# Feed-forward chunks of 12, 12, 10 and 10 blocks, and a pair of fp32 matmuls behind each feed-forward's first norm

## The chip, the core and the metric

The kernel runs on one core of a Trainium2 chip. The metric is the device time of one launch in microseconds. PE is the matrix engine (TensorE; PEld is its weight load), DVE, ACT and POOL are the vector, scalar and GpSimd engines, SP is the engine from whose queue most transfers start.

## The reference

One step of a small hybrid decoder: a prompt of 256 positions and 8 samples of 4 positions, 288 token columns in all, width 2048, all in fp32.

```
x = x + 1/2 * SwiGLU_1(rmsnorm(x))            # FFN1, d_ff = 5632
z = rmsnorm(x) @ w_in                         # mixer: state-space group and attention group
x = x + w_out @ concat(rmsnorm(y_ssm), rmsnorm(y_attn))
x = x + 1/2 * SwiGLU_2(rmsnorm(x))            # FFN2
swiglu(x) = (silu(x @ w_gate) * (x @ w_up)) @ w_down
```

The two feed-forwards, FFN1 and FFN2, are three quarters of the work. Their 5632 hidden columns are 44 blocks of 128.

## The kernel before, in words

Tokens are columns. `x[0..15]` are 16 tiles of 128 x 288, resident. A product of fp32 precision is made of three fast matmuls (fp32r): every weight piece `raw` is split into a high part `wh` (ACT, line 88) and a low part `wl` (DVE, line 89), every activation likewise (`xh`, `xl` of the normed input; `hh`, `hl` of the hidden blocks), and `mm3` issues wh by the high tile (L272), wh by the low tile (L273), wl by the high tile (L274) for each block of 128 rows. So the moving operand goes high, low, high, then on to the next block.

SBUF places are set by the pools. A tile of 288 floats is 1152 bytes per partition. `xh0` to `xh15` lie one behind the other, then the 128-byte tile `gap_x`, then `xl0` to `xl15`. The hidden blocks live in a ring of 14 `hh` tiles and a ring of 14 `hl` tiles, with the 128-byte tile `gap_r` between the two rings.

Order is written by hand. `Weights` streams a list of pieces: 512 KB pieces of gate and up weights (8 blocks, 24 matmuls), and pieces of the down weights. `next()` hands out one piece, a slot: it splits two pieces ahead, issues loads up to five ahead on SP's queue (5 `raw` buffers, 3 each of `wh` and `wl`), and runs whatever other work `at` or `spread` put at that slot, ahead of the slot's matmuls. A feed-forward goes in four chunks: `gu` of 11 blocks (4 pieces each: gate and up, two halves), the first `gu` of the next chunk, then `down` of the chunk: for each of the 16 output tiles d a PSUM tile gets 6 blocks from one piece and 5 from the next, and DVE adds it to x (L327).

The norm is applied late: `Hold` runs it some slots into the feed-forward (`first` is 10 in FFN1, 2 in FFN2): one fp32 matmul of `ones` by the sum of squares `acc` (L206), then DVE computes the row factor `R` (L200), and the evictions held up till then follow one a slot. The PSUM tiles, all named `main`, go round eight banks.

Into FFN1, from slot 24 on, the tables of the state-space part are spread (`precompute`), eight times `tile_tables`: two groups of four transposes (L556), and one or two slots later a pair of fp32 matmuls of 256 columns (L562):

```
for i, xx in ((0, xr), (1, xi)):
    pe.matmul(ps[:, :256], rep[i].rearrange("p q g c -> p (q g c)"), xx[:, :, 1:5, :],
              start=i == 0, stop=i == 1)
```

FFN2 has no such other work. In each feed-forward the slots count 304 pieces.

Of the kernel before, what the change touches and what calls it, by code (L numbers as in the profile page):

```python
# [10 lines left out]
F32 = mybir.dt.float32  # L11
# [6 lines left out]
P = 128  # L18
D = 2048
KT = D // P  # L20
# [5 lines left out]
N = T * W1  # L26
DFF = 5632
NF = DFF // P
CH = 11
NCK = NF // CH  # L30
HALF = 8 * P
EPS = 1e-6
NH = 16
# [8 lines left out]
def heads_of(i):  # L42
    kvp, g = divmod(i, 4)
    return (2 * kvp) * 4 + g, (2 * kvp + 1) * 4 + g
# [72 lines left out]
def tile_hymba_step(ctx, tc, io):  # L117
    nc = tc.nc
    act, dve, pool_e, pe, sp = nc.scalar, nc.vector, nc.gpsimd, nc.tensor, nc.sync
# [5 lines left out]
    pm = ctx.enter_context(tc.tile_pool(name="pm", bufs=8, space=PSUM))  # L125
# [4 lines left out]
    pieces = []  # L130

    def ffn_units(l):
        seq = []
        for c in range(NCK):
            for f in range(CH):
                if not (c > 0 and f == 0):
                    seq.append(("gu", c * CH + f))
            if c + 1 < NCK:
                seq.append(("gu", (c + 1) * CH))
            seq.append(("down", c))  # L140
        return seq

    def ffn_pieces(l):
        gu, dn = io["w_gu%d" % l], io["w_dn%d" % l]
        for kind, j in ffn_units(l):
            if kind == "gu":
                for s in range(2):
                    for hf in range(2):
                        pieces.append(gu[j, s, hf])
            else:  # L150
                for d in range(KT):
                    pieces.append(dn[j, d, :, :6 * P])
                    pieces.append(dn[j, d, :, 6 * P:])

    ffn_pieces(0)
    pieces[:6] = [pieces[i] for i in (0, 2, 4, 1, 3, 5)]
    MIX0 = len(pieces)
# [7 lines left out]
    W = Weights(nc, wp, pieces)  # L165
# [8 lines left out]
    ones = cp.tile([P, P], F32, name="ones")  # L174
    acc = cp.tile([P, N], F32, name="acc")
    R = cp.tile([P, N], F32, name="R")
# [91 lines left out]
    def mm3(ps, wh, wl, kts, rh, rl, first, last):  # L268
        n = len(kts)
        for a, k in enumerate(kts):  # L270
            s = slice(a * P, (a + 1) * P)
            pe.matmul(ps, wh[:, s], rh[k], start=first and a == 0, stop=False)  # L272
            pe.matmul(ps, wh[:, s], rl[k], start=False, stop=False)  # L273
            pe.matmul(ps, wl[:, s], rh[k], start=False, stop=last and a == n - 1)  # L274

    def projs(n):

        ps = [pm.tile([P, 512], F32, name="main") for _ in range(n)]
        for hf in range(2):
            for p_ in ps:  # L280
                wh, wl = W.next()
                mm3(p_[:, :N], wh, wl, range(8 * hf, 8 * hf + 8), xh, xl, hf == 0, hf == 1)
        return ps

    def proj():
        return projs(1)[0]

    def ffn(l, post, hp, first):
        HH, HL = {}, {}
        hold = Hold(W.i + first)  # L290
        early = [] if l else projs(3)

        def gate(f, pg, s2):
            t1 = tp.tile([P, N], F32, name="t1")
            s1 = tp.tile([P, N], F32, name="s1")
            dve.tensor_tensor(t1, pg[:, :N], R, op=ALU.mult)  # L296
            act.activation(s1, t1, AF.Silu)  # L297
            pool_e.tensor_tensor(s2, s1, R, op=ALU.mult)  # L298

        def up(f, pu, s2):  # L300
            h = tp.tile([P, N], F32, name="h")
            hh = hp.tile([P, N], F32R, name="hh")
            if f == 0:
                hp.tile([P, 32], F32, name="gap_r", bufs=1)
            hl = hp.tile([P, N], F32R, name="hl")
            dve.tensor_tensor(h, pu[:, :N], s2, op=ALU.mult)  # L306
            act.copy(hh, h)  # L307
            dve.tensor_tensor(hl, h, hh.bitcast(F32), op=ALU.subtract)  # L308
            HH[f % CH, f // CH], HL[f % CH, f // CH] = hh, hl

        def gu(f):
            s2 = tp.tile([P, N], F32, name="s2")
            pg = early.pop(0) if early else proj()
            hold(lambda: gate(f, pg, s2))
            pu = early.pop(0) if early else proj()
            hold(lambda: up(f, pu, s2))

        def down(c):
            rh = {k: HH.pop((k, c)) for k in range(CH)}
            rl = {k: HL.pop((k, c)) for k in range(CH)}  # L320
            for d in range(KT):
                ps = pm.tile([P, 512], F32, name="main")
                wh, wl = W.next()
                mm3(ps[:, :N], wh, wl, range(6), rh, rl, True, False)
                wh, wl = W.next()
                mm3(ps[:, :N], wh, wl, range(6, CH), rh, rl, False, True)
                dve.scalar_tensor_tensor(x[d], ps[:, :N], 0.5, x[d], op0=ALU.mult, op1=ALU.add)  # L327
                if c == NCK - 1:
                    post(d)

        for kind, j in ffn_units(l):
            (gu if kind == "gu" else down)(j)

# [779 lines left out]
def token_columns(xp, xs):  # L1113

    s = xs[:, ::-1].transpose(1, 0, 2)
    p = xp.reshape(NCH, T, -1)[:, ::-1].transpose(1, 0, 2)
    return np.concatenate([s, p], axis=1).reshape(N, -1)
# [38 lines left out]
def layout(a):  # L1156
    A = {k: np.asarray(v) for k, v in a.items()}
    c = np.ascontiguousarray
    o = {}
    xt = token_columns(A["x_prompt"][0], A["x_sample"])  # L1160
    o["x"] = c(xt.T.reshape(KT, P, N))

    def kblocks(w):

        n = w.shape[1] // P
        return w.reshape(2, 8, P, n, P).transpose(3, 0, 2, 1, 4).reshape(n, 2, P, 8 * P)

    for l, nm in enumerate(("ffn1", "ffn2")):
        g, u = kblocks(A[nm + "_w_gate"][0]), kblocks(A[nm + "_w_up"][0])
        o["w_gu%d" % l] = np.stack([g, u], 1)  # L1170
        w = A[nm + "_w_down"][0].reshape(NCK, CH, P, KT, P)
        o["w_dn%d" % l] = c(w.transpose(0, 3, 2, 1, 4).reshape(NCK, KT, P, CH * P))
    w = A["w_in"][0]
    qcols = np.concatenate([np.r_[64 * h:64 * h + 64] for i in range(8) for h in heads_of(i)])
    cols = np.concatenate([np.arange(2048, 2176), np.arange(1024), np.arange(2176, 2560), 1024 + qcols])
    o["w_in"] = c(kblocks(w[:, cols]))
    w = A["w_out"][0][np.concatenate([np.arange(1024), 1024 + qcols])]
    o["w_out"] = c(w.reshape(2, 8, P, KT, P).transpose(0, 3, 2, 1, 4).reshape(2, KT, P, 8 * P))

    def gcol(v):  # L1180
        return v.reshape(-1, P).T

    o["gains"] = c(np.concatenate(
        [gcol(A["ffn1_norm"][0]), gcol(A["mix_norm"][0]), gcol(A["ffn2_norm"][0]),
         gcol(A["ssm_out_norm"][0]), gcol(A["attn_out_norm"][0][qcols]),
         np.tile(A["q_norm"][0], 2)[:, None], np.tile(A["k_norm"][0], 2)[:, None]], 1))

    def pairs(v):

        return v.reshape((32, 2, 64) + v.shape[2:]).swapaxes(0, 1).swapaxes(1, 2).reshape(  # L1190
            (P, 32) + v.shape[2:])

    dt = np.repeat(A["ssm_log_dt"][0][:, None], 64, 1)
    dco = A["ssm_D"][0].reshape(8, P).T
    o["ssm_prm"] = c(np.concatenate([pairs(A["ssm_A_re"][0]), pairs(A["ssm_A_im"][0]), pairs(dt),
                                     dco], 1))
    o["ssm_bc"] = c(np.stack([pairs(A["ssm_B_re"][0]), pairs(A["ssm_B_im"][0]),
                              pairs(A["ssm_C_re"][0].swapaxes(1, 2)),
                              pairs(A["ssm_C_im"][0].swapaxes(1, 2))], 1))
    o["h0"] = c(np.stack([pairs(A["state_ssm_%s" % r][0].transpose(1, 2, 0)) for r in ("re", "im")], 1))  # L1200
    glu = np.zeros((8, 8, 16, 8, 16), np.float32)
    for g in range(8):
        glu[:, g, :, g, :] = A["ssm_w_glu"][0].reshape(8, 8, 16, 16)[:, g]
    o["w_glu"] = glu.reshape(8, P, P)
    o["ssm_cst"], o["mix_cst"], o["ident"] = constants()
    sk = A["sinks"][0]
    sp_ = np.concatenate([np.r_[sk[list(heads_of(i))], sk[list(heads_of(i))]] for i in range(8)])
    g = (np.arange(P) // 4) % 4
    ss = np.stack([sk[kv * 4 + g] for kv in range(4)], 1)
    o["sinks"] = c(np.concatenate([np.tile(sp_[None], (P, 1)), ss], 1))  # L1210
    o["cache_k"], o["cache_v"] = A["cache_k"], A["cache_v"]
    o["cache_kT"] = c(A["cache_k"][0].reshape(NB, WIN, 2, P).transpose(2, 3, 0, 1))
    o["cache_vr"] = c(A["cache_v"][0].reshape(NB, WIN, 2, P).transpose(2, 1, 0, 3))
    return o
# [44 lines left out]
```

## Time and profile before

| | |
|---|---|
| median of 3 runs | 2023.21 us (2022.99 to 2023.37) |
| the profiled execution: time, span | 2021.75 us, 2020.0 us |
| granted PE clock | 1.00 throughout |
| PE, DVE, ACT, POOL busy | 99%, 60%, 42%, 15% of the span |
| HBM traffic | 178 GB/s over the span |
| FFN1; mixer; FFN2 (PE's first matmul of each) | 6.3; 862.5; 1172.4 us |

The profiled execution's time is 1.75 us more than its span. Everything below is read against that one execution and then carried over to the median, which is 1.5 us higher. A matmul here is shown with a duration of some 0.29 us while the next starts some 0.13 us behind it, so they overlap: what counts is the distance of their starts, which a number of matmuls in a window of known length gives.

### The profile page before, as it was taken

Reading aid. Unit: us, or ns where it says so; the run is one execution under the profiler, and the core shown is the slowest. Engines: PE = TensorE matmul, PEld = TensorE weight load, DVE = VectorE, ACT = ScalarE, POOL = GpSimd, SP = SyncE. Lnnn points to the kernel's source line nnn. Section 1 sums busy time; section 2 is a strip of 40 time slices with the busy share of each in tenths; the row PEclk is TensorE's granted clock in tenths of the full one; section 3 lists DMA queues with packets and bytes.
Section 4 is the critical chain, followed back from the end, with each engine's and each line's share of the span. In section 5 each row is a group of like instructions: output and inputs, shape, how many; then the busy total and the mean of one; then the engine's idle time right before and its main releaser. Section 6 shows DMA issues by size and latency. Waiting matters only on the chain.

```text
span 2020.0 us, 37616 instructions
## 1 busy us (share of the span) xinstructions
PE 2004.1 (99%) x15248; PEld 1992.0 (99%) x15248; DVE 1218.3 (60%) x1874; ACT 852.3 (42%) x1334; POOL 298.8 (15%) x450
## 2 busy tenths in 40 slices
PE   8999999999999999999999999999999999999999
PEld 8999999999999999999989999999999999999999
DVE  5677666666656655677787974455445444454454
ACT  5433443444444433533476543333333333333332
POOL 3100011001110000212477720000000000000000
PEclk9999999999999999999999999999999999999999
DMA  7555656565656564678733555555555655465554
GB/s 237 189 161 151 215 158 200 175 207 163 201 173 197 180 199 147 215 238 273 238 126 127 165 161 165 161 151 182 166 168 146 188 164 162 146 180 170 164 158 149
DMA packets 122622, 359.04 MB, mean 178 GB/s; under 512 B 22448, under 2 KB 30256, under 8 KB 121264
## 3 DMA queue, kind: packets, MB, share of 16 engines
q1 hardware_dynamic: 114672, 340.81, 53.7%
q10 hardware_dynamic: 7776, 15.83, 2.3%
q8 instruction: 119, 1.95, 0.4%
q14 instruction: 55, 0.45, 0.1%
HBM read 338.40 MB, written 20.22 MB: 178 GB/s over the span
## 4 chain that ended last, share of the span: by engine, by line
PE 94%; POOL 2%; DVE 2%; DMA 1%; issue 0%; ACT 0%; SPq 0%; POOLq 0%; ACTq 0%; DVEq 0%
PE main L272 30%; PE main L274 30%; PE main L273 30%; POOL acc L190 1%; PE main L723 1%; DVE wl L89 1%; DMA yd<-yg 0%; PE main L556 0%; PE main L562 0%; DMA x<-in_x 0%; PE main L765 0%; PE main L764 0%; PE main L763 0%; DMA raw<-in_w_gu 0%; POOL rq_t L891 0%
## 5 line engine op out<-in xcount | busy, mean ns | idle before, releaser
L89 DVE TENSOR_TENSOR wl<-raw,wh 128x1024 fp32r<-128x1024 f32 (+2 forms) x680 | 757.8, 1115 | 539.8 <-ACT wh L88 535.6
L272 PE MATMUL main<-xh,wh 128*128 128x288 f32 x3136 | 931.0, 297 | 6.9 <-ACT xh L180 6.3
L274 PE MATMUL main<-xh,wl 128*128 128x288 f32 x3136 | 925.8, 295 | 1.3 <-DVE wl L89 1.3
L273 PE MATMUL main<-xl,wh 128*128 128x288 f32 x3136 | 925.4, 295 | 0.6 <-DVE xl L181 0.6
L88 ACT CAST wh<-raw 128x1024 fp32r<-128x1024 f32 (+2 forms) x680 | 643.0, 946 | 614.1 <-PE main L273 406.9
L272 PEld LDWEIGHTS main<-xh,wh 128*128 128x128 f32 x3136 | 591.9, 189 | 8.1 <-ACT xh L180 6.3
L274 PEld LDWEIGHTS main<-xh,wl 128*128 128x128 f32 x3136 | 591.7, 189 | 2.0 <-DVE wl L89 2.0
L273 PEld LDWEIGHTS main<-xl,wh 128*128 128x128 f32 x3136 | 591.9, 189 | 1.4 <-DVE xl L181 1.0
L272 PE MATMUL main<-hh,wh 128*128 128x288 f32 x1664 | 494.1, 297 | 0.0
L273 PE MATMUL main<-hl,wh 128*128 128x288 f32 x1664 | 490.9, 295 | 0.3 <-DVE hl L674 0.3
L274 PE MATMUL main<-hh,wl 128*128 128x288 f32 x1664 | 491.0, 295 | 0.0
L273 PEld LDWEIGHTS main<-hl,wh 128*128 128x128 f32 x1664 | 313.9, 189 | 0.7 <-DVE hl L674 0.6
L272 PEld LDWEIGHTS main<-hh,wh 128*128 128x128 f32 x1664 | 313.3, 188 | 0.4
L274 PEld LDWEIGHTS main<-hh,wl 128*128 128x128 f32 x1664 | 313.6, 188 | 0.0
L298 POOL TENSOR_TENSOR s<-s,R 128x288 f32<-128x288 f32 x88 | 71.5, 813 | 1253.7 <-ACT s L297 1253.7
L297 ACT ACTIVATE s<-t 128x288 f32<-128x288 f32 x88 | 39.2, 445 | 237.5 <-DVE t L296 237.5
L307 ACT CAST hh<-h 128x288 fp32r<-128x288 f32 x88 | 38.1, 433 | 239.6 <-DVE h L306 239.6
L327 DVE SCALAR_TENSOR_TENSOR x<-main,x 128x288 f32<-128x288 f32 x128 | 58.4, 456 | 51.0 <-PE main L274 49.1
L306 DVE TENSOR_TENSOR h<-main,s 128x288 f32<-128x288 f32 x88 | 40.2, 457 | 77.0 <-PE main L274 76.8
L296 DVE TENSOR_TENSOR t<-main,R 128x288 f32<-128x288 f32 x88 | 40.2, 457 | 63.6 <-PE main L274 63.1
L308 DVE TENSOR_TENSOR hl<-h,hh 128x288 fp32r<-128x288 f32 x88 | 40.4, 459 | 44.0 <-ACT hh L307 44.0
L190 POOL TENSOR_TENSOR acc<-acc,sq 128x288 f32<-128x288 f32 x45 | 48.5, 1079 | 52.5 <-ACT sq L186 51.1
(264 smaller groups left out, 890.1 us busy)
## 6 DMA issues: line engine op xcount, KB each, us to landing
raw<-in_w_gu SPq DMA_DIRECT2D x352, 512.0 KB, 3.5
raw<-in_w_dn SPq DMA_DIRECT2D x128, 384.0 KB, 3.1
raw<-in_w_dn SPq DMA_DIRECT2D x128, 320.0 KB, 2.9
raw<-in_w_in SPq DMA_DIRECT2D x40, 512.0 KB, 4.5
raw<-in_w_out SPq DMA_DIRECT2D x32, 512.0 KB, 3.4
mats<-stage ACTq DMA_DIRECT2D x8, 1536.0 KB, 7.0
mb<-mats SPq DMA_DIRECT2D x8, 768.0 KB, 5.7
ma<-mats SPq DMA_DIRECT2D x8, 512.0 KB, 4.3
```

The lines of the kernel that those rows point to most:

```text
L88: self.nc.scalar.copy(wh[:, :n], t[:, :n])
L89: self.nc.vector.tensor_tensor(wl[:, :n], t[:, :n], wh[:, :n].bitcast(F32), op=ALU.subtract)
L190: eng.tensor_tensor(acc, acc, sq, op=ALU.add)
L272: pe.matmul(ps, wh[:, s], rh[k], start=first and a == 0, stop=False)
L273: pe.matmul(ps, wh[:, s], rl[k], start=False, stop=False)
L274: pe.matmul(ps, wl[:, s], rh[k], start=False, stop=last and a == n - 1)
L296: dve.tensor_tensor(t1, pg[:, :N], R, op=ALU.mult)
L297: act.activation(s1, t1, AF.Silu)
L298: pool_e.tensor_tensor(s2, s1, R, op=ALU.mult)
L306: dve.tensor_tensor(h, pu[:, :N], s2, op=ALU.mult)
L308: dve.tensor_tensor(hl, h, hh.bitcast(F32), op=ALU.subtract)
L327: dve.scalar_tensor_tensor(x[d], ps[:, :N], 0.5, x[d], op0=ALU.mult, op1=ALU.add)
```

## The change

The four chunks have 12, 12, 10 and 10 blocks. A down piece carries half a chunk, 6 or 5 blocks, and lies contiguous in its own array in HBM; before, the pieces were the first 768 and the last 640 columns of rows of 1408. And a function `gap` runs eight slots behind the first norm of each feed-forward: two fp32 matmuls of `ones` by 256 columns of `R` into a PSUM tile that nothing reads.

```diff
-CH = 11
-NCK = NF // CH
+CHS = (12, 12, 10, 10)
+NCK = len(CHS)
+C0 = [sum(CHS[:c]) for c in range(NCK)]
...
             else:
                 for d in range(KT):
-                    pieces.append(dn[j, d, :, :6 * P])
-                    pieces.append(dn[j, d, :, 6 * P:])
+                    pieces.append(dn[j][d, 0])
+                    pieces.append(dn[j][d, 1])
...
     def ffn(l, post, hp, first):
         HH, HL = {}, {}
+        w0 = W.i
         hold = Hold(W.i + first)
...
         def down(c):
-            rh = {k: HH.pop((k, c)) for k in range(CH)}
-            rl = {k: HL.pop((k, c)) for k in range(CH)}
+            n = CHS[c]
+            rh = {k: HH.pop(C0[c] + k) for k in range(n)}
+            rl = {k: HL.pop(C0[c] + k) for k in range(n)}
             for d in range(KT):
                 ps = pm.tile([P, 512], F32, name="main")
                 wh, wl = W.next()
-                mm3(ps[:, :N], wh, wl, range(6), rh, rl, True, False)
+                mm3(ps[:, :N], wh, wl, range(n // 2), rh, rl, True, False)
                 wh, wl = W.next()
-                mm3(ps[:, :N], wh, wl, range(6, CH), rh, rl, False, True)
+                mm3(ps[:, :N], wh, wl, range(n // 2, n), rh, rl, False, True)
...
+        def gap():
+
+            ps = pm.tile([P, 512], F32, name="main")
+            for i in range(2):
+                pe.matmul(ps[:, :256], ones, R[:, 8:264], start=i == 0, stop=i == 1)
+
+        W.at(w0 + first + 8, gap)
```

Lines move by one to ten: `mm3`'s L272 to L274 are L273 to L275 now, the table's L556 and L562 are L566 and L572, the new pair is L338.

Where it stands on PE in FFN2, first the pair. Before, at slot 10 of FFN2 (`xh15` ends a block's second gate piece, `xh0` begins its first up piece; the numbers tell tiles of one name apart):

```order
L272 MATMUL main_14501<-xh15_102,wh_14464 128x288
L273 MATMUL main_14501<-xl15_119,wh_14464 128x288
L274 MATMUL main_14501<-xh15_102,wl_14465 128x288
L272 MATMUL main_14567<-xh0_87,wh_14502 128x288
L273 MATMUL main_14567<-xl0_104,wh_14502 128x288
L274 MATMUL main_14567<-xh0_87,wl_14503 128x288
```

The same place on PE now, with the pair as one row of two:

```order
L273 MATMUL main_14504<-xh15_102,wh_14467 128x288
L274 MATMUL main_14504<-xl15_119,wh_14467 128x288
L275 MATMUL main_14504<-xh15_102,wl_14468 128x288
L338 MATMUL main_14577<-R_124,ones_122 128x256 x2
L273 MATMUL main_14570<-xh0_87,wh_14505 128x288
L274 MATMUL main_14570<-xl0_104,wh_14505 128x288
```

Nothing else moved there: the pair stands between two pieces, ahead of `xh0`.

Second, on PE the seam between output tiles 0 and 1 in the first down of FFN2. Before, `hh_15701` is the chunk's block 10 and `hh_14368` its block 0:

```order
L272 MATMUL main_15840<-hh_15701,wh_15804 128x288
L273 MATMUL main_15840<-hl_15702,wh_15804 128x288
L274 MATMUL main_15840<-hh_15701,wl_15805 128x288
L272 MATMUL main_15887<-hh_14368,wh_15841 128x288
L273 MATMUL main_15887<-hl_14370,wh_15841 128x288
```

Now, on PE at the same seam, `hh_15841` is block 11 and `hh_14371` block 0:

```order
L273 MATMUL main_15980<-hh_15841,wh_15944 128x288
L274 MATMUL main_15980<-hl_15842,wh_15944 128x288
L275 MATMUL main_15980<-hh_15841,wl_15945 128x288
L273 MATMUL main_16030<-hh_14371,wh_15981 128x288
L274 MATMUL main_16030<-hl_14373,wh_15981 128x288
```

An output tile ends on a block with an odd number in its chunk now (11 or 9), where it ended on an even one (10).

Third, on PE in FFN1's last down, behind the pair of the seventh table, whose slot is the same in both. Before, a second half of 5 blocks follows it, from the chunk's block 6 (`hh_6229`) on:

```order
L562 MATMUL main_7386<-xr_6943,rep0_245 128x256
L562 MATMUL main_7386<-xi_6944,rep1_246 128x256
L272 MATMUL main_7349<-hh_6229,wh_7321 128x288
L273 MATMUL main_7349<-hl_6230,wh_7321 128x288
L274 MATMUL main_7349<-hh_6229,wl_7322 128x288
```

Now, on PE, a second half of 5 blocks follows too, but from the chunk's block 5 (`hh_6478`) on:

```order
L572 MATMUL main_7507<-xr_7042,rep0_245 128x256
L572 MATMUL main_7507<-xi_7043,rep1_246 128x256
L273 MATMUL main_7473<-hh_6478,wh_7445 128x288
L274 MATMUL main_7473<-hl_6479,wh_7445 128x288
L275 MATMUL main_7473<-hh_6478,wl_7446 128x288
```

The tables' work keeps its slots; the pieces at these slots are other ones.

More of the change, by code (lines that the diff above doesn't have):

```diff
@@ L134, in ffn_units @@
         for c in range(NCK):
-            for f in range(CH):
+            for f in range(CHS[c]):
                 if not (c > 0 and f == 0):
-                    seq.append(("gu", c * CH + f))
+                    seq.append(("gu", C0[c] + f))
             if c + 1 < NCK:
-                seq.append(("gu", (c + 1) * CH))
+                seq.append(("gu", C0[c + 1]))
             seq.append(("down", c))
@@ L143, in ffn_pieces @@
     def ffn_pieces(l):
-        gu, dn = io["w_gu%d" % l], io["w_dn%d" % l]
+        gu, dn = io["w_gu%d" % l], [io["w_dn%d_%d" % (l, c)] for c in range(NCK)]
         for kind, j in ffn_units(l):
@@ L308, in up @@
             dve.tensor_tensor(hl, h, hh.bitcast(F32), op=ALU.subtract)
-            HH[f % CH, f // CH], HL[f % CH, f // CH] = hh, hl
+            HH[f], HL[f] = hh, hl
         def gu(f):
@@ L1170, in layout @@
         o["w_gu%d" % l] = np.stack([g, u], 1)
-        w = A[nm + "_w_down"][0].reshape(NCK, CH, P, KT, P)
-        o["w_dn%d" % l] = c(w.transpose(0, 3, 2, 1, 4).reshape(NCK, KT, P, CH * P))
+        w = A[nm + "_w_down"][0].reshape(NF, P, KT, P)
+        for i, n in enumerate(CHS):
+            v = w[C0[i]:C0[i] + n].reshape(2, n // 2, P, KT, P)
+            o["w_dn%d_%d" % (l, i)] = c(v.transpose(3, 0, 2, 1, 4).reshape(KT, 2, P, n // 2 * P))
     w = A["w_in"][0]
```

## The prediction

> **What bounds the kernel now.** I read the page first, for the busy shares and the chain that ended last.
>
> ```profile
> span 2020.0 us, 37616 instructions
> PE 2004.1 (99%) x15248; PEld 1992.0 (99%) x15248; DVE 1218.3 (60%) x1874; ACT 852.3 (42%) x1334; POOL 298.8 (15%) x450
> ...
> PE 94%; POOL 2%; DVE 2%; DMA 1%; issue 0%; ACT 0%; SPq 0%; POOLq 0%; ACTq 0%; DVEq 0%
> ```
>
> PE is the bound. The other engines have spare time, and PE's own list of waits, read second, holds nothing worth removing:
>
> ```profile
> engine line waited for: us in total, times, longest us
> PE main L272 <- ACT xh L180: 6.3, 1, 6.3
> PE main L274 <- DVE wl L89: 1.3, 3, 0.9
> ```
>
> 6.3 us is the start of the program; all the rest is small. So time can only come from the pace at which PE takes its 14,400 split-weight matmuls of 288 columns. A busy share can't show that, since these matmuls overlap. A count in a window can. Third, PE alone in stretches of the two feed-forwards (columns: window, its length, PE busy and number of matmuls):
>
> ```profile
> core 0: us, PE busy (x), PEclk, DMA share, GB/s
> 70.22:166.22 96.00, 96.00 (x722) 1.00 0.54 174
> 287.82:356.20 68.38, 68.38 (x528) 1.00 0.59 192
> 356.90:363.40 6.50, 6.50 (x51) 1.00 0.47 144
> 364.53:379.99 15.46, 15.46 (x121) 1.00 0.42 118
> 380.65:417.40 36.75, 36.75 (x279) 1.00 0.65 205
> 488.90:557.30 68.40, 68.40 (x528) 1.00 0.59 192
> 565.70:593.64 27.94, 27.94 (x217) 1.00 0.59 190
> 593.64:597.93 4.29, 4.29 (x35) 1.00 0.29 91
> 598.99:622.10 23.11, 23.11 (x177) 1.00 0.61 175
> 689.55:792.33 102.78, 102.78 (x792) 1.00 0.56 175
> 793.13:844.40 51.27, 51.27 (x388) 1.00 0.64 201
> 1204.83:2016.32 811.49, 811.49 (x6097) 1.00 0.54 164
> 1607.44:1748.24 140.80, 140.80 (x1059) 1.00 0.51 161
> 1946.27:2016.32 70.05, 70.05 (x529) 1.00 0.56 165
> ```
>
> A window that opens on a start also counts the one or two matmuls still running, so I take off up to two. The reader is to see two paces at the same granted clock of 1.00 and the same shapes. Slow: 96.00/720 = 133.3 ns in gate and up pieces, 70.05/528 = 132.7 ns in down. Fast: 68.38/526 = 130.0 ns, again in 488.90, 565.70, 593.64 and 689.55. FFN2 is slow throughout: 811.49/6096 = 133.1 ns.
>
> Fourth, what stands where the pace changes. The fast stretches begin behind one thing, the pair of fp32 matmuls of 256 columns in `tile_tables`:
>
> ```profile
> 286.65 0.29 PE L274 MATMUL main<-xh,wl 128*128 128x288 f32 x1
> 286.78 0.59 PE L562 MATMUL main<-xr,rep 128*128 128x256 f32 x2
> 287.21 0.59 PE L562 MATMUL main<-xi,rep 128*128 128x256 f32 x2
> 287.45 0.48 PE L272 MATMUL main<-xh,wh 128*128 128x288 f32 x1
> 287.78 0.29 PE L273 MATMUL main<-xl,wh 128*128 128x288 f32 x1
> ```
>
> The transposes of the next table end it (356.90, 132.7 ns). So does something inside down. At 597.93, after exactly 33 fast matmuls of down, the steps become 0.14 and 0.13:
>
> ```profile
> 597.80 0.29 PE L274 MATMUL main<-hh,wl 128*128 128x288 f32 x1
> 597.93 0.29 PE L272 MATMUL main<-hh,wh 128*128 128x288 f32 x1
> 598.07 0.29 PE L273 MATMUL main<-hl,wh 128*128 128x288 f32 x1
> 598.20 0.30 PE L274 MATMUL main<-hh,wl 128*128 128x288 f32 x1
> ```
>
> My reading is about where the moving operand starts. A tile of 288 floats is 1152 bytes, nine times 128, and `gap_x` and `gap_r` put 128 bytes between the high and the low tiles. So successive moving operands start alternately on an even and an odd multiple of 128 bytes: xh0, xl0, xh0, xh1, and on. An output block of down has 11 blocks times 3 = 33 matmuls, an odd number, so the last operand of one d and the first of the next start on the same parity. That is the point at 597.93. Entering down, xh15 is followed by a ring place: the chunk that begins at block 22 (place 8 of 14) kept the pace at 593.64, those at 11 and 33 (places 11 and 5) lost it at 380 and 792.33. Place parity explains all three. A slow stretch goes on through any number of correct alternations (1607.44, 1056 matmuls), so it takes both an entry and no repeat.
>
> **The change part by part.**
>
> *Chunks of 12, 12, 10, 10.* Nothing is added: 3 x 44 x 16 matmuls of down as before, and as many pieces of 768 and of 640 columns. An output block has 36 or 30 matmuls, and chunks begin at blocks 0, 12, 24, 34, all even, so no two neighbours of a feed-forward share a parity. By itself this buys nothing in a slow stretch, and may cost: without the repeats down could fall to 133.3 from 132.7, 0.6 ns each.
>
> *The pair.* It stands in front of xh0, an even place. It reads `R[:, 8:264]`; adding up the tiles of the pools, that starts 192 bytes past a multiple of 256, as xr and xi do. Nothing is read back, and its operand is old:
>
> ```profile
> 52.57 0.46 DVE L200 SCALAR_TENSOR_TENSOR R<-rt,R 128x288 f32<-128x288 f32 x1
> ```
>
> R is done at 53.0, and the pair's place in FFN1 is at 70.2, so PE doesn't wait. It takes one PSUM bank of eight out of turn; the tile eight places earlier was read four pieces before. Its price by the rows of the table pair: from 286.78 to 287.78 PE did the pair and one ordinary matmul, 1.00 - 0.13 = 0.87 us. Two pairs: +1.7.
>
> What no row shows is whether this pair starts the fast pace too, as its moving operand is one run of 256 columns and xr's is four of 64. The bounds are none of it and all of it. The one nearer row against is the single fp32 matmul of the norm:
>
> ```profile
> 1178.76 0.65 PE L206 MATMUL main<-acc,ones 128*128 128x288 f32 x2
> ```
>
> Behind it FFN2 stays slow. It has one matmul, 288 columns and another start (acc at 32 past 256). The pair shares the count, the columns and the start with L562, so I take all of it.
>
> *FFN2.* From the pair on 6096 matmuls: 811.49 against 6096 x 130.0 = 792.5, so -19.0. Nothing in FFN2 interrupts them.
>
> *FFN1.* From 70.22 there are 3792 gate and up matmuls, of which 526 + 120 + 526 + 215 + 790, some 2180, are fast already, and 2112 of down, some 60 fast. Afterwards slow: between the transposes and the pair of each table, 5 x 48 of gate and up and 36 + 36 + 30 of down, and behind the seventh table 315 of down and 24, because there the pair is followed by an odd place (the second half of a 10-block output). Newly fast: 3792 - 2180 - 264 = 1348 x 3.33 = 4.5 us, and 2112 - 60 - 417 = 1635 x 2.7 = 4.4. The 417 slow ones of down may lose 0.2. Together -8.7. The first two mixer pieces, 48 matmuls, give another 0.2.
>
> *Feeding the faster PE.* Beside the fast stretch and in the last, busiest down of FFN1:
>
> ```profile
> core 0: us, PE busy (x) PEld busy (x) DVE busy (x) ACT busy (x) POOL busy (x), PEclk, DMA share, GB/s
> 689.55:792.33 102.78, 102.78 (x792) 102.78 (x792) 52.83 (x68) 41.26 (x61) 6.49 (x8) 1.00 0.56 175
> 793.13:862.50 69.37, 69.37 (x524) 69.37 (x523) 42.12 (x62) 37.45 (x63) 14.28 (x14) 1.00 0.66 204
> ```
>
> DVE at 61% and ACT at 54% there have room for 2% more pace. 13 of 14 ring places are now held at a down instead of 12; the place that the next block writes is free either way. The down weights now lie contiguous; I cost that at nothing, by the gate and up pieces, contiguous already, which land in similar time for more bytes:
>
> ```profile
> raw<-in_w_gu SPq DMA_DIRECT2D x352, 512.0 KB, 3.5
> raw<-in_w_dn SPq DMA_DIRECT2D x128, 384.0 KB, 3.1
> raw<-in_w_dn SPq DMA_DIRECT2D x128, 320.0 KB, 2.9
> ```
>
> **Sum.** -19.0 - 8.7 - 0.2 + 1.7 = -26.2 us. The profiled execution took 2021.75 (span 2020.0 and 1.75 around it) and would take 1995.6. The median shown is 2023.21, 1.5 above it, so I predict 2023.2 - 26.2 = 1997.0.
>
> **Rivals.**
>
> *The pair doesn't start the fast pace.* Then FFN1 speeds up behind the first table's pair only: 528 of gate and up (1.8 us) and some 1330 of down (3.6); 2112 + 720 slow matmuls of down lose up to 0.6 ns (1.7); the pairs cost 1.7. Net -2.0: 2021.2. For it: the norm's row. Against it: the likeness to L562.
>
> *It starts, but the pace is lost in down, or to one late operand.* No row shows more than 33 fast matmuls of down in a row, and in FFN2 nothing brings the pace back. Lost at the first d: FFN2 gains 1008 x 3.33 = 3.4, FFN1 about 1100 x 3.33 + 0.4 = 4.1, less 1.7 and up to 0.8 of slower down: 2018. Lost halfway through FFN2: 2023.2 - 26.2 + 9.5 = 2006.5. Against it: PE waited for nothing in FFN2.
>
> *It works in FFN2 alone.* 19.0 and what the rep pairs give FFN1 (5.0), less 1.7: 2000.9.
>
> *The pace doesn't hang on where operands start.* If shape alone sets it and the two levels have another cause, the change is only the two pairs: 2023.2 + 1.7 = 2024.9, no change that can be told. The Trainium skill, "TensorE: Matmul & The Clock Gate", section "Back-to-back issue gap", states such a rule: a warm gap of N/2.4 + 2.5 ns, by the columns N alone, an estimate of 122.5 ns for 288; by its "Part 2: What happens when you issue a matmul" the weight load takes no read bandwidth from the moving operand. Rows disagree: 130.0 and 133.3 for one shape.
>
> *Slower: the contiguous weights land late.* A down piece is split in 0.84 + 0.96 us:
>
> ```profile
> L88 ACT CAST wh<-raw 128x768 fp32r<-128x768 f32 x15 | 12.5, 836 | 8.3 <-ACT sq L186 6.5 <-PE main L273 1.8
> L89 DVE TENSOR_TENSOR wl<-raw,wh 128x768 fp32r<-128x768 f32 x15 | 14.4, 958 | 4.8 <-ACT wh L88 4.8
> ```
>
> Five raw buffers hold a piece for its landing and those 1.8 us; down pieces take PE 16.5 x 0.13 = 2.14 us on average. PE waits once landing passes 5 x 2.14 - 1.8 = 8.9 us. At 10 us a piece takes 2.36, and 256 pieces cost 55: 2052. It ends above the time before from about 9.5. Against it: 3.5 us for 512 KB.
>
> **How the numbers follow.** Forecast 0.74; no start 0.07; lost on the way 0.08; FFN2 alone 0.04; shape alone 0.04; late weights 0.03. Within 0.2%, some 4 us, is about what a measurement of this kernel can't tell from no change. Faster: 0.74 + 0.08 + 0.04 = 0.86; same 0.11; slower 0.03. If every matmul behind the pairs ran fast the table stretches would give 2 more, 1994.9, so the low end is 1994. The high end, 2006, takes in FFN2 alone and a loss up to halfway: 0.74 + 0.04 + 0.03 = 0.81.
>
> **What the changed profile would show.** FFN2 from its pair to the end at some 793 us instead of 811, any window of it at 130.0 ns, down included; a step to the next d without 0.14; FFN1 slow only between transposes and rep pair and behind the seventh table. A window of FFN2 at 133 behind the pair would refute the entry, one that turns slow at a d boundary the parity, and rows of PE waiting for wh, wl or raw the feeding.

## The result, and the profile after

The changed kernel takes 1999.68 us (median of 4 runs, 1997.81 to 1999.87) beside 2023.29 us for the kernel before on the same chip: a ratio of 0.9882, 95% interval 0.987 to 0.9894, so 23.6 us less. 1997.0 was predicted, with a range of 1994 to 2006. The profiled execution took 1999.87 us (span 1998.1), 21.9 us less than that of before.

The page's span, busy shares and the shares of the chain that ended last, after:

```profile
span 1998.1 us, 37634 instructions
PE 1980.5 (99%) x15256; PEld 1968.0 (98%) x15256; DVE 1219.0 (61%) x1874; ACT 852.0 (43%) x1334; POOL 296.0 (15%) x450
PE 96%; DMA 1%; POOL 1%; DVE 0%; SPq 0%; ACT 0%; issue 0%; POOLq 0%; ACTq 0%; DVEq 0%
```

PE is busy for the same 99% and carries even more of the chain. A reader who looks at shares alone sees no change. PE's list of waits is as short as before; its two longest rows, and the two for transfers of the mixer, of which the one for `U` is new:

```profile
engine line waited for: us in total, times, longest us
PE main L273 <- ACT xh L181: 6.4, 1, 6.4
PE main L275 <- DVE wl L90: 2.2, 3, 0.9
PE main L794 <- DMA gl<-in_w_glu: 1.2, 1, 1.2
PE main L733 <- DMA U<-ud: 1.2, 1, 1.2
```

No wait for `raw`, and those for `wl` are the three short ones in the first 39 us. What changed is the number of matmuls in a window. PE alone in stretches of the changed kernel, each opened just behind a pair of fp32 matmuls (window, its length, PE busy and number of matmuls, of which one or two were still running when it opened):

```profile
core 0: us, PE busy (x), PEclk, DMA share, GB/s
72.10:217.70 145.60, 145.60 (x1123) 1.00 0.55 174
224.50:284.20 59.70, 59.70 (x450) 1.00 0.61 202
292.50:360.90 68.40, 68.40 (x528) 1.00 0.58 192
437.40:490.80 53.40, 53.40 (x403) 1.00 0.63 206
639.70:684.60 44.90, 44.90 (x339) 1.00 0.69 221
693.00:864.30 171.30, 171.30 (x1320) 1.00 0.60 192
1202.20:1994.43 792.23, 792.23 (x6096) 1.00 0.54 168
```

The last row is the result: FFN2 from its pair to its end, down included, 792.23 us instead of 811.49, 6095 starts 129.98 ns apart. The first row is the same behind FFN1's pair, as far as the first table's transposes: 145.60/1121 = 129.9 ns. 292.50 and 693.00 are fast behind table pairs. But 224.50, 437.40 and 639.70, behind the pairs of the first, fourth and seventh table, hold 59.70/449 = 133.0, 53.40/401 = 133.2 and 44.90/338 = 132.8 ns: slow.

By stage, from PE's first matmul of one to that of the next, in the two profiled executions:

| stage | before, us | after, us | change | predicted, with the pairs |
|---|---|---|---|---|
| FFN1 | 856.3 | 851.8 | -4.4 | -8.7 + 0.87 = -7.8 |
| mixer | 309.8 | 310.5 | +0.7 | -0.2 |
| FFN2 | 844.0 | 825.7 | -18.3 | -19.0 + 0.87 = -18.1 |

### The profile page after: what moved, and what is told of

It reads as the page before. It is cut to its first block, busy times and chain, and to the rows that moved or that the text cites. A ratio compares the mean times of both kernels' runs of the same rounds, so it can differ in the third digit from the quotient of the medians.

```text
span 1998.1 us, 37634 instructions
## 1 busy us (share of the span) xinstructions
PE 1980.5 (99%) x15256; PEld 1968.0 (98%) x15256; DVE 1219.0 (61%) x1874; ACT 852.0 (43%) x1334; POOL 296.0 (15%) x450
## 4 chain that ended last, share of the span: by engine, by line
PE 96%; DMA 1%; POOL 1%; DVE 0%; SPq 0%; ACT 0%; issue 0%; POOLq 0%; ACTq 0%; DVEq 0%
PE main L273 31%; PE main L275 31%; PE main L274 31%; POOL acc L191 1%; PE main L733 1%; DMA yd<-yg 0%; PE main L566 0%; PE main L572 0%; DMA x<-in_x 0%; PE main L988 0%; DMA raw<-in_w_gu 0%; PE main L775 0%; PE main L774 0%; PE main L956 0%; PE main L773 0%; PE main L975 0%
## 5 line engine op out<-in xcount | busy, mean ns | idle before, releaser
L273 PE MATMUL main<-xh,wh 128*128 128x288 f32 x3136 | 924.4, 295 | 6.7 <-ACT xh L181 6.4
L275 PE MATMUL main<-xh,wl 128*128 128x288 f32 x3136 | 919.0, 293 | 2.2 <-DVE wl L90 2.2
L274 PE MATMUL main<-xl,wh 128*128 128x288 f32 x3136 | 918.4, 293 | 0.6 <-DVE xl L182 0.6
L273 PEld LDWEIGHTS main<-xh,wh 128*128 128x128 f32 x3136 | 589.5, 188 | 8.0 <-ACT xh L181 6.4
L275 PEld LDWEIGHTS main<-xh,wl 128*128 128x128 f32 x3136 | 589.3, 188 | 3.0 <-DVE wl L90 2.9
L274 PEld LDWEIGHTS main<-xl,wh 128*128 128x128 f32 x3136 | 589.5, 188 | 1.4 <-DVE xl L182 1.0
L273 PE MATMUL main<-hh,wh 128*128 128x288 f32 x1664 | 489.8, 294 | 0.0
L274 PE MATMUL main<-hl,wh 128*128 128x288 f32 x1664 | 487.9, 293 | 0.3 <-DVE hl L684 0.3
L275 PE MATMUL main<-hh,wl 128*128 128x288 f32 x1664 | 487.8, 293 | 0.0
L274 PEld LDWEIGHTS main<-hl,wh 128*128 128x128 f32 x1664 | 312.6, 188 | 0.7 <-DVE hl L684 0.5
L273 PEld LDWEIGHTS main<-hh,wh 128*128 128x128 f32 x1664 | 312.5, 188 | 0.5 <-DVE t L1095 0.2
L275 PEld LDWEIGHTS main<-hh,wl 128*128 128x128 f32 x1664 | 312.5, 188 | 0.0
```

## The experiments

Each run answers one question on the theory of the prediction: a pace of 130.0 ns is entered behind a pair of fp32 matmuls and kept as long as successive moving operands start alternately on even and odd multiples of 128 bytes. Edits are against the changed kernel.

### The new chunks without the pair

```diff
-        W.at(w0 + first + 8, gap)
```

> The chunks of 12, 12, 10 and 10 without the pair. My theory (even chunks keep the fast pace, but only a pair of fp32 matmuls starts it): FFN2 at 133.3 ns throughout, 6096 matmuls in some 812.8 us, and FFN1 fast only behind table pairs; about 2022 to 2024 us, no change that can be told. Rival (the chunks themselves bring the pace): FFN2 near 793 us and about 2000 us.

2020.12 us, ratio 0.9983 (0.9974 to 0.9993). FFN2 without a pair, one window from its first norm to its end:

```profile
1177.10:2015.20 838.10, 838.10 (x6288) 1.00 0.53 164
```

838.10/6287 = 133.3 ns throughout: the even chunks by themselves bring FFN2 nothing. In the profiled executions FFN1 is 2.4 us shorter than before, where the table pairs start stretches that now last, and FFN2 1.2 longer, its down at 133.3 instead of 132.7. One of these stretches stands behind the first table's pair, which starts nothing in the changed kernel (224.50 above) and does here, with all operands at the same SBUF places:

```profile
227.65:285.90 58.25, 58.25 (x451) 1.00 0.61 208
```

58.25/448 = 130.0 ns. So for this pair something decides that isn't where the operands start.

### The pair without the new chunks

```diff
-CHS = (12, 12, 10, 10)
+CH = 11
```

with the old cut of the down weights and the pair kept.

> The pair with the old chunks of 11. My theory (an odd number of matmuls in an output tile repeats a start and ends the fast pace): FFN2 fast from its pair to the end of the first output tile of the first down, 912 + 33 matmuls at 130.0 ns, then 133 to the end; FFN1 fast from its pair into the first down likewise; about 2019 to 2020 us. Rival (the pair alone does it): about 2000 us.

2018.60 us, ratio 0.9982 (0.9973 to 0.9992). Behind FFN1's pair, behind FFN2's, and a stretch of FFN2's first down just after that:

```profile
core 0: us, PE busy (x), PEclk, DMA share, GB/s
71.10:168.90 97.80, 97.80 (x755) 1.00 0.54 171
1203.80:1326.40 122.60, 122.60 (x946) 1.00 0.51 158
1328.00:1348.00 20.00, 20.00 (x153) 1.00 0.59 175
```

97.80/753 = 129.9 and 122.60/944 = 129.9 ns, then 20.00/151 = 132.5. The trace's own starts end the fast pace exactly after 752 and 944 steps. These are the matmuls of gate and up that were left (30 pieces of 24 = 720; 38 of 24 = 912) and the 33 of one output tile, less one: the step from the last operand of output tile 0 to the first of tile 1 is the repeated parity. Both parts of the change are needed: alone each brings some 3.5 us by its ratio, together they bring 23.6.

### Even chunks, wrong parity

`gap_x` grows to 256 bytes, so that each `xl` starts on the parity of its `xh`; a tile of 128 bytes behind `xl` keeps the rings on theirs.

```diff
-    cp.tile([P, 32], F32, name="gap_x")
+    cp.tile([P, 64], F32, name="gap_x")
     xl = [cp.tile([P, N], F32R, name="xl%d" % k) for k in range(KT)]
+    cp.tile([P, 32], F32, name="gap_z")
```

> As changed, but gap_x is 64 floats instead of 32, and 32 floats more lie behind xl so that all later tiles keep their place modulo 256 bytes. The numbers of matmuls stay even, but xh and xl of one block now start on the same parity of 128 bytes, so starts repeat all through gate and up. My theory (starts must alternate): gate and up never below 133 ns, FFN2 at 811 us or more, total 2022 to 2030 us. Rival (an even number of matmuls per output tile is what counts, wherever they start): about 2000 us with FFN2 at 130.0 ns.

2031.74 us, ratio 1.0042 (1.0027 to 1.0057). Forty pieces of gate and up in FFN2:

```profile
1655.40:1783.20 127.80, 127.80 (x960) 1.00 0.50 157
```

127.80/959 = 133.3 ns, in steps of 133 to 134 ns nearly all and none of 140, pair or not. In down the operands of this kernel still alternate, and there the first and the fourth table's pair do start the fast pace; behind the first it lasts up to the gate and up pieces:

```profile
227.40:257.50 30.10, 30.10 (x234) 1.00 0.68 235
```

30.10/232 is 129.7 ns. Shape, number and order of the matmuls are those of the changed kernel; only addresses moved. So the fast pace needs starts that alternate, and the rivals that shape alone or an even number of matmuls decides fall. FFN1 takes 863.8 us here, 7.5 more than before, since the fast stretches that it had in gate and up are gone.

### The same kernel with the pair in the middle of a piece

FFN1's pair stands after 12 matmuls of its slot, 204 behind the norm, FFN2's after 6, 198 behind it; both in front of an even place.

```diff
-        W.at(w0 + first + 8, gap)
+        W.at(w0 + first + 8, inside.__setitem__, (4, 2)[l], gap)
```

> As changed, but the pair stands inside a piece: in FFN1 behind 4 blocks (12 matmuls), in FFN2 behind 2 blocks (6 matmuls); in both the next operand starts on the even place, as behind the changed kernel's pairs. Two table pairs in down failed to start the pace behind 18 matmuls with the right start. Theory of the slow cycle (slow matmuls come in fours, three short and one long, and the pair must come at one place of the four): FFN1 behind 204 matmuls since the norm, a multiple of four, turns fast, FFN2 behind 198 stays at 133.3 ns; about 2018 us. Rival (start of the next operand alone): both fast, about 2000 us. Second rival (only a boundary of pieces will do): both slow, about 2021 us.

2019.46 us. FFN1 behind its pair, and FFN2 behind its own:

```profile
72.90:217.10 144.20, 144.20 (x1111) 1.00 0.56 175
1202.30:2014.00 811.70, 811.70 (x6090) 1.00 0.53 164
```

144.20/1110 = 129.9 and 811.70/6089 = 133.3 ns. The same two matmuls enter in one place and not in the other, for the rest of the kernel. What differs is where they fall in the slow pace's own pattern. Its steps are not equal: one of 140 ns comes after three of 131. In ns, from the start times, ahead of a pair:

```
FFN2, changed kernel         140 130 131 132 140 131 131 131 | pair   fast
FFN1, this kernel                131 132 140 131 130 132     | pair   fast
FFN2, this kernel            140 131 131 131 140 132         | pair   slow
table 1, changed kernel      140 131 130 132 140 132         | pair   slow
table 2, changed kernel      131 131 140 131 131 132         | pair   fast
table 1, same_parity             131 131 140 131 131 132     | pair   fast
table 1, chunks_alone            130 132 140 131 131 131     | pair   fast
```

The pair enters where the long step is the fourth from last ahead of it, and not where it is the second from last. The start times of all fourteen traces agree: of these pairs, 96 have the long step fourth from last while PE runs without a wait, and all of them enter; 27 have it second, third or fifth from last, and none does. It is no count of matmuls as such: the first table's pair stands 18 matmuls behind the transposes in the changed kernel, in `same_parity` and in `chunks_alone`, and only enters in the last two, where the long step falls otherwise. What sets the long step's place behind the transposes is open.

### The failed table pairs, one to three slots later

The pairs of the first, fourth and seventh table come 1, 1 and 3 slots later (36, 36 and 60 matmuls behind the transposes instead of 18, 18 and 15); later steps of a table keep their number of slots.

```diff
+            late = {0: 1, 3: 1, 6: 3}.get(j, 0)
+            for _ in range(late):
+                yield
             ps = pa.tile([P, 512], F32, name="main")
...
-            yield
-            yield
+            for _ in range(max(0, 2 - late)):
+                yield
```

It was run twice, each time with the changed kernel beside it on the same chip.

> As changed, but the table pairs of the first, fourth and seventh table come 1, 1 and 3 slots later, so that 36, 36 and 60 matmuls lie between the transposes and the pair (multiples of four, where it was 18, 18 and 15) and an even place follows. Theory of the slow cycle: all eight table pairs start the pace; some 432 + 384 + 294 matmuls at 130.0 instead of 133.3 ns, 3.7 us less than the changed kernel, about 1996. Rival (a pair in down starts the pace or not by chance): no steady gain, within 1 us of the changed kernel.

> The changed kernel once more, beside the next two on the same chip. Theory: 23 to 25 us below the kernel before; two of the table pairs in down (first and fourth) and the seventh fail to start the pace and leave some 449, 401 and 338 matmuls of FFN1 at 133.3 ns. If a run happens to be some 2 us faster than the others, one or two of the first two pairs have caught.

1998.37 us (ratio 0.9868, 0.9852 to 0.9883) beside 1999.30 (0.9876, 0.9861 to 0.9891): all eight table pairs entered and FFN1 was 3.7 us shorter from its pair to the mixer, but in the profiled run the mixer took 316.0 us instead of 313.1. Whether a shorter FFN1 lengthens the mixer was open, so both were run again.

> The kernel of pairs_moved again: the changed kernel with the pairs of the first, fourth and seventh table 1, 1 and 3 slots later, where they had not started the fast pace before. Theory: 431, 383 and 317 matmuls at 130.0 instead of 133.3 ns, (431 + 383 + 317) x 3.33 ns = 3.8 us less than changed_third in the first feed-forward and in the whole run, ratio to the kernel before 0.9858 to 0.9870 beside 0.9876 to 0.9888. Rival (the next stage gives it back: its loads are issued by time spent and land later against its matmuls): the first feed-forward 3.7 us shorter, the mixer 2 to 4 us longer, whole runs within 1 us of changed_third.

> The changed kernel again, beside pairs_moved_2 on the same chip: 1997.5 to 2000.5 us at a granted clock of 1.0, ratio 0.987 to 0.989; first feed-forward with three slow stretches of 449, 401 and 338 matmuls behind the pairs of the first, fourth and seventh table, second feed-forward at 130.0 ns from its pair to its end; mixer 310 to 313 us.

1995.60 us (1994.52 to 1996.69; ratio 0.9861, 0.9845 to 0.9877) beside 1999.49 (1998.27 to 2004.0; 0.9885, 0.9868 to 0.9902). The three stretches, of the moved pairs, and the mixer:

```profile
core 0: us, PE busy (x), PEclk, DMA share, GB/s
225.90:281.90 56.00, 56.00 (x433) 1.00 0.59 211
437.40:487.10 49.70, 49.70 (x385) 1.00 0.63 215
642.00:683.10 41.10, 41.10 (x319) 1.00 0.68 236
853.60:1165.00 311.40, 305.72 (x2478) 1.00 0.57 191
```

and of the changed kernel beside it:

```profile
core 0: us, PE busy (x), PEclk, DMA share, GB/s
223.00:282.60 59.60, 59.60 (x450) 1.00 0.59 203
436.00:489.20 53.20, 53.20 (x401) 1.00 0.60 206
639.20:684.10 44.90, 44.90 (x340) 1.00 0.66 223
856.80:1168.30 311.50, 305.49 (x2477) 1.00 0.58 191
```

56.00/431, 49.70/383 and 41.10/317 are 129.7 to 129.9 ns, where 59.60/448, 53.20/399 and 44.90/338 are 132.8 to 133.3. The mixer is the same, 311.4 and 311.5, so a shorter FFN1 doesn't lengthen it as such; the first time the granted clock was low for 10.2 us of it (last section). The gain of 3.9 us here is the 1131 x 3.33 = 3.8 expected, and every run of this kernel lies below every one of the changed kernel beside it. By their intervals the two ratios still touch; the three stretches don't leave room for doubt. This version beats both kernels.

PE's instructions in order of time ahead of the first table's moved pair; the step of 0.14 from 224.33 to 224.47 is the long one, then three of 0.13 lead to the pair:

```profile
224.33 0.30 PE L275 MATMUL main<-hh,wl 128*128 128x288 f32 x1
224.47 0.29 PE L273 MATMUL main<-hh,wh 128*128 128x288 f32 x1
224.60 0.29 PE L274 MATMUL main<-hl,wh 128*128 128x288 f32 x1
224.73 0.29 PE L275 MATMUL main<-hh,wl 128*128 128x288 f32 x1
224.86 0.59 PE L575 MATMUL main<-xr,rep 128*128 128x256 f32 x2
```

### Pairs earlier still

The moved table pairs, and the pairs behind the norms at slot `first` + 4 (FFN1) and + 2 (FFN2).

```diff
-        W.at(w0 + first + 8, gap)
+        W.at(w0 + first + (2 if l else 4), gap)
```

> As the kernel with moved table pairs, and the pairs behind the norms come 4 slots (FFN1) and 2 slots (FFN2) behind the norm instead of 8, 96 and 48 matmuls behind it, both multiples of four. Theory: 96 and 144 more matmuls at 130.0 ns, 0.8 us less again. Rival: PE waits for a PSUM bank or for R so early, and the pace is lost at the wait: in FFN2 up to 19 us more.

2017.84 us, ratio 0.9968 (0.9958 to 0.9978). FFN1 was fast from 57.4 us on. In FFN2 the pair met a row factor that was not there yet:

```profile
1182.85 1.81 PE L338 MATMUL main<-R,ones 128*128 128x256 f32 x4 [1.89 <-DVE R L201]
1184.10 0.80 PE L273 MATMUL main<-xh,wh 128*128 128x288 f32 x1
1184.70 0.44 PE L274 MATMUL main<-xl,wh 128*128 128x288 f32 x1
1184.94 0.44 PE L275 MATMUL main<-xh,wl 128*128 128x288 f32 x1
```

and the clock behind it, with the rest of FFN2:

```profile
core 0: us, PE busy (x), PEclk, DMA share, GB/s
1182.85:1186.30 3.45, 3.45 (x12) 0.54 0.02 5
1186.60:2017.30 830.70, 830.70 (x6232) 1.00 0.49 163
```

PE stood for 1.89 us, the granted clock was 0.54 on average over the next 3.45 us, and most of the pair fell into that. The pace afterwards is 830.70/6231 = 133.3 ns to the end. A wait of 2 us there costs 20 (1998.37 without it on the same chip). The place in the pattern was the right one, the long step fourth from last ahead of the wait; whether it was the wait itself or the clock during the pair isn't told apart by this run.

### Which part of the pair does it

Three kernels change what stands in the pair's place; the results are read by nothing in all of them.

```diff
             for i in range(2):
-                pe.matmul(ps[:, :256], ones, R[:, 8:264], start=i == 0, stop=i == 1)
+                pe.matmul(ps[:, :256], ones, R[:, :256], start=i == 0, stop=i == 1)
```

in FFN1, and a single matmul of 256 columns in FFN2:

> As changed, but FFN1's pair reads R from its column 0 (32 bytes earlier), and in FFN2 one matmul of 256 columns stands for the pair. Theory A (the start place of the pair's own operand decides): FFN1 stays at 133.3 ns up to the table, 3.7 us more. Theory B (the time that the pair takes against the slow cycle decides): FFN1 fast at 130.0 ns. FFN2 by both: one matmul takes half as long and ends at another place of the cycle, so FFN2 stays slow, 19 us more less 0.4: about 2018 us by B, 2022 by A. Rival for FFN2 (any fp32 matmul of 256 columns will do): FFN2 at 130.0 ns, about 1999 us.

2023.0 us. FFN1's pair entered (1121 starts at 130.0 ns; the first window's last 0.7 us are transposes), so the start of its operand is not what matters; FFN2's single matmul did not:

```profile
71.00:217.00 146.00, 146.00 (x1126) 1.00 0.52 173
1205.50:2018.00 812.50, 812.37 (x6093) 1.00 0.49 164
```

The time alone would point to theory A. By stages it doesn't: against `changed_again` on the same chip FFN1 is 0.2 us shorter, FFN2 19.9 longer, and the mixer 2.2, where PE waits 4.0 us for transfers instead of 2.4 (the granted clock was 0.5 for 6.8 us there in both).

Then four matmuls of 128 columns in FFN1 and one of 512 in FFN2, which take PE as long as the pair:

> In the changed kernel the first feed-forward's pair becomes four fp32 matmuls of 128 columns, and the second's one fp32 matmul of 512 columns, at the same places in the order; all results are still read by nothing. Theory (it is TensorE standing some 0.86 us, 2 x 430 ns, on fp32 work in the right place of the four-matmul slow cycle that leaves the fast pace behind, not two matmuls of 256 columns as such): both feed-forwards go at 130.0 ns behind them, 1997 to 2001 us. Rival (the form of the pair is needed): the stage that rejects its replacement stays at 133.3 ns, so 6095 x 3.33 ns = 20 us more for the second feed-forward (about 2018 to 2021 us), and about 3.7 us more for the first (its 1121 matmuls to the first table's transposes).

2027.0 us; neither entered. The second ordinary start came 0.99 us behind the first of the 512 columns, as behind the pair, and 1.02 behind that of the four.

```profile
71.00:220.40 149.40, 149.40 (x1123) 1.00 0.51 169
1209.10:2021.70 812.60, 812.60 (x6096) 1.00 0.49 164
```

149.40/1121 and 812.60/6095 are 133.3 ns. Against `changed_third` on the same chip FFN1 is 4.0 us longer and FFN2 20.3; the mixer's 3.1 more go with a granted clock of 0.5 for 6.8 us there. The theory that it is the time on fp32 work falls. Last, two matmuls of 128 columns in FFN1 and three of 256 in FFN2:

> In the changed kernel the first feed-forward's pair becomes two fp32 matmuls of 128 columns and the second's three of 256, at the same places; nothing reads the results. same_time showed that the time alone (0.99 us to the second start behind) does not start the fast pace. Theory A (what counts is two matmuls, or four passes, whatever their width): first feed-forward fast behind its pair (1121 matmuls at 130.0 ns), second slow, 6095 x 3.33 = 20 us more: 2018 to 2020 us. Theory B (what counts is passes of 256 columns, two matmuls or more): first feed-forward slow to the first table's transposes (+3.7 us), second fast: 2002 to 2004 us. Theory C (only exactly two of 256 do it): both slow, 2021 to 2024 us.

2021.6 us, and neither entered again:

```profile
70.10:219.50 149.40, 149.40 (x1123) 1.00 0.51 170
1205.80:2016.30 810.50, 810.50 (x6081) 1.00 0.49 164
```

So of what was tried, only two matmuls of 256 columns start the fast pace. All these stood at one place of the pattern, the long step fourth from last ahead of them, and each form was run once; whether another form enters at another place wasn't tried. What in the pair does it is open.

## Why the prediction was right, and where a term was off

- **The entry.** "The pair shares the count, the columns and the start with L562, so I take all of it" held, on the unknown that decided most of the sum. Of the three likenesses the start was not needed (`pair_operand`), while the count and the columns were, at this place of the pattern (`pair_operand`, `same_time`, `pair_sizes`). The norm's single matmul was a poor guide: a single one of 256 columns doesn't enter either. That both new pairs stood where a pair enters was luck: the prediction didn't look at the place in the slow pattern, and 6 matmuls further on FFN2's pair starts nothing (`pair_inside`).
- **The parity.** Shown from both sides: the fast pace ends on the first repeat, to the matmul (`pair_alone`), and can't live where every block repeats (`same_parity`). The gap of N/2.4 + 2.5 ns that the prediction quotes from the Trainium skill ("TensorE: Matmul & The Clock Gate", section "Back-to-back issue gap") stands there for an isolated matmul; for a stream with weight loads the section lets both set the spacing, so it was no rule for this stream.
- **FFN2, -19.0.** Measured 811.49 - 792.23 = 19.3 from the pair on. Nothing interrupted it, as said. Without a pair its down goes at 133.3 instead of 132.7, the cost that the prediction named (`chunks_alone`).
- **The pairs, +1.7.** The second ordinary start comes 0.99 us behind the pair's first in both feed-forwards, where it would have come 0.13 behind: 0.86 each, 1.7 in all.
- **Feeding.** PE waits for no `raw`; the down pieces still land in 3.0 us at the median. The rival of late weights didn't occur.
- **FFN1, -8.7: the term that was mis-sized.** With its pair it should have given -7.8 and gave -4.4. The step that failed is that every table pair but the seventh would enter. The first and the fourth did not: 449 + 401 = 850 matmuls at 133.3 that were counted as fast, 850 x 3.33 = 2.8 us. Ahead of both, the long step is the second from last now. The prediction knew two conditions (an entry and no repeat); the third, the place in the slow pattern, was in the trace of before and was not looked for: the fourth table's pair, at 422.75 us, has the long step fifth from last there and starts nothing. That the place is the cause is shown: moved by one slot, both enter and the time comes back (`pairs_moved_2`), and with the long step fourth from last the first enters unmoved (`chunks_alone`). The seventh failed as foretold; its pair was in front of an odd place and also out of the pattern, and the runs don't tell these apart.
- **The rest of the miss.** 0.7 us were lost before FFN1's pair (64.7 us from PE's first matmul to the pair instead of 64.0), where the waits for `wl` are 2.2 instead of 1.3 us. The mixer took 0.7 more, -0.2 expected; other runs of the changed kernel at the same clock have 311.5, so this is within what runs differ by, and its cause stays open. 2.8 + 0.7 + 0.9, less 0.1 that FFN2 gave beyond the forecast, make the 4.3 by which the profiled execution missed 1995.6. Against the median the miss is 2.7, since the 1.5 us between profiled execution and median, carried over from before, didn't recur.

## What to carry to other kernels

Where PE is busy 99% of the time, count its matmuls in windows: two paces for one shape at one granted clock, here 130.0 and 133.3 ns, are time that no wait and no busy share shows. Such a pace may have conditions on addresses and on order that can be read from where it changes; write down every condition the trace shows for both outcomes, the failed entries too, before counting on it in a new place. And when two edits each bring a few us alone and 24 together, as here, neither is worth judging by itself.

## What the runs showed of the hardware that was not expected

- The slow pace is a pattern of four, steps of 140, 131, 131 and 131 ns (533.3 for four matmuls of 288 columns), and the fast one 130.0 on average, in steps of 132 and 128 by turns (`after`, FFN2 behind its pair); whether two fp32 matmuls of 256 columns lead from one to the other depends on where in the four they come. One matmul of 256, three of 256, two of 128, four of 128 and one of 512 didn't do it at the one place where they were tried.
- After 1.89 us without work the granted clock was 0.54 on average for 3.45 us in the middle of a run (`pairs_moved_early`). The length of a wait alone doesn't decide it: 2.03 us in the mixer of `changed_third` left the clock at 1.00.
- The mixer is where executions of one kernel differed: in six of the fourteen traces the granted clock was 0.5 for 3.4 to 10.2 us there, between 923 and 946 us, during a wait of PE for a transfer or within 2.1 us behind one. That of `pairs_moved`, to be read beside the two mixer rows of `pairs_moved_2` and `changed_third` above:

```profile
852.40:1168.40 316.00, 310.27 (x2479) 0.98 0.56 188
```

Its granted clock is 0.98 on average instead of 1.00 (0.5 for 10.2 us, from 0.2 us behind a wait of 2.1 us for `gl` on), and it is 4.6 us longer than the 311.4 of the same kernel on another chip, more than the gain that it hid. For a change of a few us the clock of each stage is to be compared before the times are.
